# Residual rows and half of the gated tiles turned by VectorE through DRAM, with permuted features and channels, the decay's sums a step later, and one load for the small vectors

## The chip, the cores and the metric

The kernel runs on one core of a Trainium2 chip. The metric is the device time of one execution in microseconds (us). Inputs and weights lie in the core's HBM, laid out by the host beforehand (the function `_layout` of the kernel file), which isn't part of the time.

## The reference

Two layers over 256 context and 256 latent tokens of width 1024. Layer 0 mixes tokens with a Conformer convolution, layer 1 with a bidirectional chunkwise mLSTM (4 heads of 512); each is followed by a squared-ReLU MLP. Every sub-layer is modulated by adaLN vectors of `c` (latent) or `c_ctx` (context) and normalised behind its residual. Cut to what matters here:

```python
def conformer_conv(u, rows, w_pw1, b_pw1, w_dw, b_dw, ln_g, ln_b, w_pw2, b_pw2):
    a = u @ w_pw1 + b_pw1
    a = a[..., :CONV_DIM] * jax.nn.sigmoid(a[..., CONV_DIM:])     # the gated tiles
    ...                                                           # depthwise convolution of 31 taps along tokens
    a = jax.nn.silu(layer_norm(a + b_dw, ln_g, ln_b))
    return a @ w_pw2 + b_pw2

def mlstm_chunk_scan(q, k, v, i_pre, f_pre, state):
    lf = jax.nn.log_sigmoid(f_pre)
    ...
        bcum = jnp.cumsum(lfc, axis=-1)                           # the decay's sums
...
    h = layer_norm(ALPHA * h + g1 * y, ln1_g[i], ln1_b[i])        # ALPHA * h: the residual
```

## The kernel before, in words

Activations lie with features on the 128 partitions and tokens along the free axis: 8 tiles of 128 features by 512 tokens (256 context, 256 latent). Each fp32 product is three fp32r products of high and low halves (`mm3`: high by high, high by low, low by high, L182, L185, L186; `mm3t` with the operands' roles swapped, L213 to L215). The high half of a weight block of 128x1024 is a cast on ScalarE (L151), the low half a subtract on VectorE (L152); raw weights come in loads of 1 MB (`raw_load`, L145) on SyncE's queue SP, with three buffers.

The order of the work within an engine is fixed when the program is built, from the order of the code and the scheduler's own estimates; `tc.issue_after` ties an instruction behind another one. Each engine, and each queue, works in its own order.

**The start.** SP loads the small vectors `vecs` in two pieces: 64 columns ahead of all weights (L117, 32 KB), and the other 344 behind two feature tiles' loads (L657, 172 KB). The adaLN weights follow, and TensorE multiplies them with the conditioning at L344, once for each of eight feature tiles, in turn with the first four output tiles of the first pointwise product.

**The gated tiles.** The first pointwise product (`pw1_epi`) gives 16 output tiles, a gate and an up half for each `f` of eight: the sigmoid of the gate on ScalarE (L791), then bias and product on VectorE (L795), which gives 128 channels by 512 tokens. The convolution is done as Fourier transforms along tokens, so tokens must lie on the partitions: `turn` makes four 128x128 transposes on TensorE (L806) and one copy to the rows tile `A` by ScalarE (L807). Tiles 0 to 2 are put off to the next output tile (`turns`). The forward transform (`fwd`, L830 and L835) reads channels 0 to 511 of `A` (tiles 0 to 3) in its first half and 512 to 1023 in its second. The spectrum of the taps (L741) is a product with a table `tab` of cosines, which VectorE computes in the same stretch (L706 to L715).

**The residual rows.** Layer 1 continues in rows (tokens on partitions) after its output projection. Between the z projection (`up_z`) and the x projection (`up_x`), ScalarE scales and shifts the eight feature tiles (L1199), TensorE turns them (16 transposes, L1202), ScalarE copies them to a rows tile (L1204) and writes this to DRAM (`r_dr`, L1205, 1 MB). It is loaded again (L1573) at the output gate's second head half, `(h, d) == (0, 1)`. The epilogue of `up_x` is `x_epi`.

**The decay.** A string of names sets the order of the mLSTM's parts: a generator of main work (the output gate `gate_o`, attention `attend`, output projection `down`) and one of side work (`decay`, `guards`, `weights`), of which some steps are taken per step of the main one. A `yield` is the end of a step. `decay` makes `lf`, the log-sigmoid of the forget gates (last of it L1421), then on TensorE its sums (L1435 with triangles, L1436 with ones), and from these the running maximum `negm`. `gate_o` multiplies with `wo` in the three products of L213 to L215, and adds its bias on VectorE (L1588).

Of the kernel before, what the change touches and what calls it, by code (L numbers as in the profile page):

```python
# [21 lines left out]
C = 256  # L22
# [49 lines left out]
def hybrid_kernel(ctx: ExitStack, tc: tile.TileContext, xT, vecs_d, wdw_d, ada0_w, ada_w, wg_d, pw1a, pw1, pw2, w1_0, w2_0,  # L72
# [12 lines left out]
    def nm(s):  # L85
        uid[0] += 1
        return f"{s}_{uid[0]}"
# [3 lines left out]
    def tmp(tag, dt=F32):  # L91
        return tp.tile([P, T], dt, tag=tag, name=nm(tag), bufs={"E": 4, "S": 2, "L": 2, "F": 1}[tag])
# [8 lines left out]
    def psum(tag="mm"):  # L101
        return pp.tile([P, 512], F32, tag=tag, name=nm(tag), bufs={"mm": 3, "ln": 2, "fl": 1, "cv": 2}[tag])
# [551 lines left out]
    start1(0)  # L654
    idle(spare, 5)
    start0(1)
    nc.sync.dma_start(vecs[:, NV0:], vecs_d[:, NV0:])  # L657
    for f in range(DT):
        start2(f, (0,))
        if f + 1 < DT:  # L660
# [118 lines left out]
                              qtr.rearrange("p (b j c) -> p j b c", b=4, j=4)[:, :, :, 0:16])  # L779


    A = padp.tile([P, 4, D], F32, name="A")
# [18 lines left out]
    turns = []  # L801

    def turn(f, a):
        tr = psum("ln")
# [106 lines left out]
    def pw1_next(m, ps):  # L911
        while turns:
            turns.pop(0)()
        if m == 3:
            first.extend(ada_load(0, 4))
            ada_g1.mm(first, range(4))
        if m == 11:
            ada_s2.mm(half + ada_load(0, 6 + ada_s2.n, halves=(1,)))
            with tc.issue_after(mark["gate"]):
                nc.scalar.activation(warm, eps, AF.Sqrt)  # L920
        if m in (5, 6):
            with tc.issue_after(lastmm[0]):
# [265 lines left out]
    for _ in side:  # L1188
        pass

    def rows_tile():
        return xp.tile([P, 2, D], F32, tag="res", name=nm("res"), bufs=1)

    r_dr = dp.tile([P, 2, D], F32, name="r_dr")
    R = rows_tile()
    for f in range(0, DT, 2):
        t, tr = tmp("S"), psum("cv")
        for i in range(2):
            nc.scalar.activation(t[:, i * C:(i + 1) * C], x[f + i][:, HI], AF.Identity, scale=al[:, 0, f + i:f + i + 1],  # L1199
                                 bias=al[:, 1, f + i:f + i + 1])  # L1200
            for tt in range(2):
                nc.tensor.transpose(tr[:, tt * C + i * P:tt * C + (i + 1) * P],  # L1202
                                    t[:, i * C + tt * P:i * C + (tt + 1) * P], ident)
# [8 lines left out]
    def x_epi(m, ps):  # L1212
        pad = B("pad5")
        nc.gpsimd.memset(pad[:, :, 0:2], 0.0)
        nc.gpsimd.memset(pad[:, :, C + 2:C + 4], 0.0)
        mid = pad[:, :, 2:C + 2]
        nc.scalar.copy(mid, s2_(ps))
        nc.scalar.dma_start(xl_dr[m // 8][:, m % 8, :], pad[:, 1, 2:C + 2])
        hi, lo = XM(F32R), (X if m % 2 else U)(F32R)
        nc.scalar.copy(hi, ps)  # L1220
        nc.vector.tensor_tensor(s2_(lo), mid, s2_(hi.bitcast(F32)), op=ALU.subtract)
        xm.append((hi, lo))
        acc, sg = tmp("E"), tmp("E")
# [4 lines left out]
        nc.scalar.activation(sg, acc, AF.Silu)  # L1228
# [163 lines left out]
    def decay(_):  # L1392
# [565 lines left out]
def _cols(v):  # L1958
    return v.reshape(-1, P).T
# [6 lines left out]
def _layout(np, i):  # L1966
    g = {k: np.asarray(v) for k, v in i.items()}
    a, turned = {}, _turned(np)
    a["xT"] = np.concatenate([g["ctx"][0], g["x"][0]], axis=0).T
    vec = {  # L1970
        "c_ctx": _cols(g["c_ctx"]), "c": _cols(g["c"][0]),
        "b_pw1": _cols(g["conv_b_pw1"][0]),
        "cln_g": _cols(g["conv_ln_g"][0]), "cln_b": _cols(g["conv_ln_b"][0]),
        "b_pw2": _cols(g["conv_b_pw2"][0]), "b_conv": _cols(g["ml_b_conv"][0]),
        "w_conv": g["ml_w_conv"][0].T.reshape(ET, P, QTAP).transpose(1, 0, 2).reshape(P, ET * QTAP),
# [15 lines left out]
    pw1 = g["conv_w_pw1"][0].reshape(D, 2, DT, P).transpose(0, 2, 1, 3)[:, :, ::-1, :].reshape(D, 2 * D)  # L1991
# [16 lines left out]
    ab = g["ada_b"][1].reshape(6, D)  # L2008
# [25 lines left out]
```

## Time and profile before

| | |
|---|---|
| median of three runs | 1662.8 us (1662.76, 1662.8, 1665.79) |
| the profiled execution | 1665.14 us, its span 1663.4 us |
| TensorE busy | 1648.7 us, 8856 matmuls |
| VectorE, ScalarE busy | 1038.1 us, 734.6 us |
| granted TensorE clock | 0.999 |
| the transposes that the change takes from TensorE | 16 at L1202 (629.1 to 633.9 us), 16 of the 32 at L806 (50.5 to 143.9 us) |
| moved by DMA | 303.70 MB |

All times of rows are microseconds from the start of the span; the span lies in an execution that takes 1.7 us more. An engine's share of the span says how far it is from being the bound. A matmul's duration contains the pipeline's length, so matmuls that follow each other overlap in the rows, and the distance of their starts is what one costs in the stream. "A<-B" is a row's output and input by the names of the program.

### The profile page before, as it was taken

The page shows a single profiled execution, that of the slowest core. Times are in us where ns is not written, and L with a number is a line of the kernel's source. Part 1 is how long each engine was busy: PE and PEld are TensorE (multiplying, and loading weights), DVE is VectorE, ACT ScalarE, POOL GpSimd, SP SyncE. Part 2 cuts the span into 40 slices and gives each one's busy share as a digit, 9 for nine tenths or more (in the row PEclk, how much of TensorE's full clock was granted, in tenths as well). Part 3 has the DMA queues.
Part 4 walks back from the last instruction along what each step waited for, and adds up shares of the span by engine and source line. Part 5 has one row for each costly group of instructions (what it writes and reads, how often), then busy time and mean ns, then how long its engine had stood idle before and what let it go on. Part 6 is the DMA issues. An engine that isn't in the chain of part 4 may idle for free.

```text
span 1663.4 us, 22731 instructions
## 1 busy us (share of the span) xinstructions
PE 1648.7 (99%) x8856; PEld 1357.6 (82%) x8856; DVE 1038.1 (62%) x1863; ACT 734.6 (44%) x1182; POOL 14.4 (1%) x64
## 2 busy tenths in 40 slices
PE   9999999999999999999999999999999999999998
PEld 6665898888888998877787899888877888878886
DVE  6554895666535765762354753553489876776677
ACT  4313573232324476652233533442477654555453
POOL 0000000000000000000000000000000000000001
PEclk9999999999999999999999999999999999999999
DMA  9555223534324065557774852554465555675552
GB/s 353 208 210 214 92 75 111 167 123 148 136 101 152 4 228 194 184 196 266 278 259 146 302 179 79 179 194 144 148 240 197 203 215 203 250 284 183 178 194 85
DMA packets 74331, 303.70 MB, mean 183 GB/s; under 512 B 7694, under 2 KB 23858, under 8 KB 44144
## 3 DMA queue, kind: packets, MB, share of 16 engines
q1 hardware_dynamic: 56368, 286.49, 49.1%
q10 hardware_dynamic: 17856, 15.77, 2.8%
q8 instruction: 69, 1.13, 0.3%
q14 instruction: 38, 0.31, 0.1%
HBM read 285.42 MB, written 16.81 MB: 182 GB/s over the span
## 4 chain that ended last, share of the span: by engine, by line
PE 95%; DVE 2%; DMA 1%; ACT 1%; issue 0%; SPq 0%; DVEq 0%; ACTq 0%
PE mm L182 18%; PE mm L185 17%; PE mm L186 17%; PE mm L197 7%; PE mm L198 4%; PE mm L215 3%; PE mm L213 3%; PE mm L214 3%; PE cv L213 2%; PE cv L215 2%; PE cv L214 2%; PE fl L344 1%; PE ln L182 1%; PE cv L860 1%; PE ln L214 1%; PE ln L185 1%
## 5 line engine op out<-in xcount | busy, mean ns | idle before, releaser
L152 DVE TENSOR_TENSOR wl<-raw,wh 128x1024 fp32r<-128x1024 f32 x344 | 418.7, 1221 | 245.5 <-ACT wh L151 233.4
L151 ACT CAST wh<-raw 128x1024 fp32r<-128x1024 f32 x344 | 358.6, 1051 | 469.3 <-PE mm L185 244.4
L185 PE MATMUL mm<-u,wh 128*128 128x512 f32 (+1 forms) x808 | 291.5, 361 | 0.2 <-DVE u L604 0.2
L182 PE MATMUL mm<-u,wh 128*128 128x512 f32 (+1 forms) x680 | 243.8, 359 | 0.0
L186 PE MATMUL mm<-u,wl 128*128 128x512 f32 (+1 forms) x680 | 241.3, 355 | 0.0
L185 PEld LDWEIGHTS mm<-u,wh 128*128 128x128 f32 x808 | 152.7, 189 | 23.2 <-issue 1.0
L182 PEld LDWEIGHTS mm<-u,wh 128*128 128x128 f32 x680 | 128.4, 189 | 24.4 <-issue 6.3
L186 PEld LDWEIGHTS mm<-u,wl 128*128 128x128 f32 x680 | 128.5, 189 | 17.8
L213 PE MATMUL mm<-wh,xl 128*128 128x512 f32 x256 | 101.0, 395 | 0.7 <-DVE og L1588 0.7
L182 PE MATMUL mm<-xm,wh 128*128 128x512 f32 x256 | 101.0, 394 | 0.0
L215 PE MATMUL mm<-wl,xl 128*128 128x512 f32 x256 | 100.0, 393 | 0.0
L214 PE MATMUL mm<-wh,xl 128*128 128x512 f32 x256 | 99.9, 390 | 0.0
L186 PE MATMUL mm<-xm,wl 128*128 128x512 f32 x256 | 99.7, 389 | 0.0
L182 PE MATMUL mm<-hid,wh 128*128 128x512 f32 (+1 forms) x256 | 93.3, 364 | 0.0
L186 PE MATMUL mm<-hid,wl 128*128 128x512 f32 (+1 forms) x256 | 92.8, 363 | 0.0
L185 PE MATMUL mm<-hid,wh 128*128 128x512 f32 (+1 forms) x256 | 92.8, 363 | 0.0
L197 PE MATMUL mm<-x,wh 128*128 128x512 f32 x232 | 81.1, 398 | 0.0
L185 PE MATMUL mm<-qq,wh 128*128 128x272 f32 x256 | 73.9, 289 | 0.0
L182 PE MATMUL mm<-qq,wh 128*128 128x272 f32 x256 | 73.5, 288 | 0.0
L186 PE MATMUL mm<-qq,wl 128*128 128x272 f32 x256 | 73.5, 288 | 0.0
L197 PE MATMUL mm<-u,wh 128*128 128x512 f32 x192 | 68.6, 399 | 0.0
L1099 DVE SCALAR_TENSOR_TENSOR x<-mm,ada,x 128x256 f32<-128x256 f32 x64 | 28.5, 479 | 63.4 <-PE mm L186 63.4
(537 smaller groups left out, 3249.4 us busy)
## 6 DMA issues: line engine op xcount, KB each, us to landing
raw<-w SPq DMA_DIRECT2D x64, 1024.0 KB, 4.9
raw<-wo SPq DMA_DIRECT2D x32, 1024.0 KB, 4.9
raw<-ada_w SPq DMA_DIRECT2D x22, 1024.0 KB, 7.0
ar<-ada_w SPq DMA_DIRECT2D x80, 256.0 KB, 3.9
raw<-wv SPq DMA_DIRECT2D x16, 1024.0 KB, 8.0
raw<-wqT SPq DMA_DIRECT2D x16, 1024.0 KB, 5.7
raw<-wq SPq DMA_DIRECT2D x16, 1024.0 KB, 5.8
raw<-wk SPq DMA_DIRECT2D x16, 1024.0 KB, 5.2
```

The lines of the kernel that those rows point to most:

```text
L151: c = nc.scalar.copy(hi, src)
L152: lastsub[0] = nc.vector.tensor_tensor(lo, src, hi.bitcast(F32), op=ALU.subtract).ins
L182: a = nc.tensor.matmul(ps, wh, xh, start=start, stop=False)
L185: nc.tensor.matmul(ps, wh, xl, start=False, stop=False)
L186: lastmm[0] = nc.tensor.matmul(ps, wl, xh, start=False, stop=stop).ins
L197: todo = [lambda s_, e_: nc.tensor.matmul(ps, wh, r[0], start=s_, stop=e_), lambda s_, e_: nc.tensor.matmul(ps[:, :n], wl, r[0][:, :n], st ...
L198: lambda s_, e_: nc.tensor.matmul(ps[:, :n], wl, r[0][:, :n], start=s_, stop=e_)]
L213: nc.tensor.matmul(ps, xh, wh, start=start, stop=False)
L214: nc.tensor.matmul(ps, xl, wh, start=False, stop=False)
L215: nc.tensor.matmul(ps, xh, wl, start=False, stop=stop)
L344: a = mark_unit[0] = nc.tensor.matmul(ps[32 * j:32 * j + 32], cs[:, kt, 14 - 2 * v:46 - 2 * v], blocks[kt], start=first and kt < 4, stop=l ...
L1099: nc.vector.scalar_tensor_tensor(res[m][:, sl_], p_, g[:, m:m + 1], res[m][:, sl_], op0=ALU.mult, op1=ALU.add)
```

## The change

Six things, in one edit. (1) Features (of `x`, of the weights that make or read them, and of the vectors) and the channels of tiles 0, 1, 4 and 5 are permuted on the host in blocks of 32. A transpose of VectorE turns each 32x32 block by itself, and in the permuted order the blocks that it leaves lie so that one strided write to DRAM puts them in their rows. (2) Tiles 0, 1, 4 and 5 aren't turned by `turn`: VectorE transposes each (`vturn3`), and after the second of a pair ScalarE's queue writes the two in four DMAs (128 KB each, in runs of 64 elements) to `a_dr`; SP (first pair) and ScalarE's queue (second pair, at output tile 8 of those that follow) load them into `A`. Tile 2 alone is put off now. (3) The eight tiles of the residual are transposed by VectorE, 128x256 each, and four DMAs write them to `r_dr`, one in each of the first four epilogues of `up_x`. (4) The rows are loaded at `(1, 1)` of the output gate. (5) Two more `yield`s stand ahead of the decay's sums. (6) `vecs` is loaded in one piece of 204 KB ahead of all weights.

```diff
@@ -113,8 +113,7 @@
 
 
     vecs = con.tile([P, NV], F32, name="vecs")
-    NV0 = _OFF["ada_b1"][0]
-    nc.sync.dma_start(vecs[:, :NV0], vecs_d[:, :NV0])
+    nc.sync.dma_start(vecs, vecs_d)
 
...
     start0(1)
-    nc.sync.dma_start(vecs[:, NV0:], vecs_d[:, NV0:])
...
+    a_dr = [dp.tile([P, 4, 2 * P], F32, name=f"a_dr{h}") for h in range(2)]
...
-        if f < 3:
+        if f == 2:
             turns.append(lambda: turn(f, a))
+        elif f % 4 > 1:
+            turn(f, a)
         else:
-            turn(f, a)
+            vturn3(f, a)
...
+    def vturn3(f, a):
+        h, m = divmod(f, 4)
+        if m == 0:
+            three.append(rows_tile().rearrange("p a b -> p (a b)")[:, 0:8 * P].rearrange("p (t q m j) -> p t q m j", q=4, m=2, j=32))
+        vk = three[-1]
+        nc.vector.transpose(vk[:, :, :, m, :], a)
+        if m == 1:
+            for r in range(4):
+                nc.scalar.dma_start(a_dr[h][:, :, r * 64:r * 64 + 64].rearrange("(q j) t x -> j t q x", j=32),
+                                    vk[32 * r:32 * r + 32].rearrange("j t q m i -> j t q (m i)"))
+            if h == 0:
+                with tc.issue_after(loaded[0]):
+                    nc.sync.dma_start(A[:, :, 0:2 * P], a_dr[0])
...
         pw1_epi(m + KO0, ps)
+        if m == 8:
+            with tc.issue_after(mark["gate"]):
+                nc.scalar.dma_start(A[:, :, 512:512 + 2 * P], a_dr[1])
...
-    R = rows_tile()
+    vr = rows_tile().rearrange("p a (b m j) -> p a b m j", m=DT, j=32)
     for f in range(0, DT, 2):
-        t, tr = tmp("S"), psum("cv")
+        t = tmp("S")
         for i in range(2):
             nc.scalar.activation(t[:, i * C:(i + 1) * C], x[f + i][:, HI], AF.Identity, scale=al[:, 0, f + i:f + i + 1],
                                  bias=al[:, 1, f + i:f + i + 1])
-            for tt in range(2):
-                nc.tensor.transpose(tr[:, tt * C + i * P:tt * C + (i + 1) * P],
-                                    t[:, i * C + tt * P:i * C + (tt + 1) * P], ident)
-        nc.scalar.copy(R[:, :, f * P:(f + 2) * P], tr.rearrange("p (t c) -> p t c", t=2))
-    nc.scalar.dma_start(r_dr, R)
+            nc.vector.transpose(vr[:, :, :, f + i, :], t[:, i * C:(i + 1) * C])
...
+        if m < 4:
+            with tc.issue_after(o.ins):
+                nc.scalar.dma_start(r_dr[:, :, m * C:(m + 1) * C].rearrange("(q j) t x -> j t q x", j=32),
+                                    vr[32 * m:32 * m + 32].rearrange("j t q m i -> j t q (m i)"))
...
+        yield
+        yield
         yield
         yield
         bps = psum("ln")
...
-            if (h, d) == (0, 1):
+            if (h, d) == (1, 1):
                 with tc.issue_after(loaded[0]):
                     nc.sync.dma_start(R, r_dr)
...
+    xs = np.arange(D).reshape(4, DT, 32).transpose(1, 0, 2).reshape(D)
+    for n in ("conv_w_pw1", "mlp_w1", "ml_w_up"):
+        g[n] = np.concatenate([g[n][:1][:, xs], g[n][1:]])
...
+    glu = np.arange(D)
+    for h in (0, 512):
+        glu[h:h + 256] = h + np.arange(256).reshape(4, 2, 32).transpose(1, 0, 2).reshape(256)
```

**TensorE at the taps.** The rows are in program order, with the kernel's line, the output and its inputs (`mm` and `ln` are accumulators, `u` the modulated input, `wh` and `wl` a weight block's halves). Before, from the last matmuls of one output tile on:

```order
L186 MATMUL mm_604<-u_427,wl_650 128x512
L182 MATMUL mm_604<-u_473,wh_649 128x512
L185 MATMUL mm_604<-u_474,wh_649 128x512
L186 MATMUL mm_604<-u_473,wl_650 128x512
L182 MATMUL mm_684<-u_154,wh_688 128x512
L741 MATMUL ln_678<-L_575,tab 128x512
L741 MATMUL ln_681<-L_575,tab 128x512
L185 MATMUL mm_684<-u_155,wh_688 128x512
```

Now, from the same place on:

```order
L181 MATMUL mm_681<-u_154,wh_685 128x512
L184 MATMUL mm_681<-u_155,wh_685 128x512
L185 MATMUL mm_681<-u_154,wl_686 128x512
L181 MATMUL mm_681<-u_196,wh_685 128x512
L184 MATMUL mm_681<-u_197,wh_685 128x512
L185 MATMUL mm_681<-u_196,wl_686 128x512
L181 MATMUL mm_681<-u_242,wh_685 128x512
L184 MATMUL mm_681<-u_243,wh_685 128x512
L185 MATMUL mm_681<-u_242,wl_686 128x512
L181 MATMUL mm_681<-u_288,wh_685 128x512
L739 MATMUL ln_675<-L_574,tab 128x512
L739 MATMUL ln_678<-L_574,tab 128x512
```

Nine more matmuls of 512 columns of the next output tile stand ahead of the taps' product with `tab` (line 741 before, 739 now). The eight transposes of tiles 0 and 1, which stood further up (between the two output tiles before), are gone.

**VectorE at the taps.** Before, from the products that complete tiles 0 and 1 (L795; 797 now) on, with the low halves of weights (L152; 151 now) and the table's steps (L711 and L712; 709 and 710 now):

```order
L710 TENSOR_SCALAR tab<-F_532 128x384
L795 SCALAR_TENSOR_TENSOR E_596<-mm_106,vecs,E_596 128x512
L795 SCALAR_TENSOR_TENSOR E_599<-cv_108,vecs,E_599 128x512
L711 TENSOR_TENSOR F_533<-tab 128x384
L152 TENSOR_TENSOR wl_650<-raw_605,wh_649 128x1024
L152 TENSOR_TENSOR wl_689<-raw_686,wh_688 128x1024
L152 TENSOR_TENSOR wl_731<-raw_686,wh_730 128x1024
L712 TENSOR_SCALAR F_532<-F_533 128x384
L706 TENSOR_SCALAR F_546<-tab 128x256
```

Now:

```order
L708 TENSOR_SCALAR tab<-F_531 128x384
L797 SCALAR_TENSOR_TENSOR E_597<-mm_106,vecs,E_597 128x512
L797 SCALAR_TENSOR_TENSOR E_602<-cv_108,vecs,E_602 128x512
L812 STREAM_TRANSPOSE res_600<-E_597 128x16x32
L812 STREAM_TRANSPOSE res_600<-E_602 128x16x32
L151 TENSOR_TENSOR wl_647<-raw_614,wh_646 128x1024
L151 TENSOR_TENSOR wl_686<-raw_683,wh_685 128x1024
L151 TENSOR_TENSOR wl_728<-raw_683,wh_727 128x1024
L709 TENSOR_TENSOR F_532<-tab 128x384
L704 TENSOR_SCALAR F_545<-tab 128x256
L710 TENSOR_SCALAR F_531<-F_532 128x384
```

Two transposes stand ahead of three weight blocks, and the step of the table that stood right behind the products (L711) has gone behind those blocks.

**The decay on TensorE.** `wh` and `wl` are the halves of a `wo` block, `xl` the tokens' inputs. Before:

```order
L213 MATMUL mm_10689<-wh_10855,xl_10672 128x512
L214 MATMUL mm_10689<-wh_10855,xl_10672 128x512
L215 MATMUL mm_10689<-wl_10856,xl_10672 128x512
L213 MATMUL mm_10690<-wh_10855,xl_10669 128x512
L214 MATMUL mm_10690<-wh_10855,xl_10669 128x512
L1435 MATMUL ln_10750<-E_10714,tri 128x4x32
L215 MATMUL mm_10690<-wl_10856,xl_10669 128x512
L1436 MATMUL ln_10750<-E_10713,ones 128x4x32
L1435 MATMUL ln_10750<-E_10714,tri 128x4x4
L1436 MATMUL ln_10750<-E_10713,ones 128x4x4
L213 MATMUL mm_10690<-wh_10855,xl_10672 128x512
```

Now, with the same sums in lines 1455 and 1456, from two matmuls before the place in the block at which they stood:

```order
L212 MATMUL mm_10670<-wh_10820,xl_10649 128x512
L213 MATMUL mm_10670<-wh_10820,xl_10649 128x512
L214 MATMUL mm_10670<-wl_10821,xl_10649 128x512
L212 MATMUL mm_10670<-wh_10820,xl_10652 128x512
L213 MATMUL mm_10670<-wh_10820,xl_10652 128x512
L214 MATMUL mm_10670<-wl_10821,xl_10652 128x512
L212 MATMUL mm_10669<-wh_10853,xl_10655 128x512
L1455 MATMUL ln_10748<-E_10694,tri 128x4x32
L213 MATMUL mm_10669<-wh_10853,xl_10655 128x512
L1456 MATMUL ln_10748<-E_10693,ones 128x4x32
L1455 MATMUL ln_10748<-E_10694,tri 128x4x4
L1456 MATMUL ln_10748<-E_10693,ones 128x4x4
```

The sums with the triangle stood behind the second matmul of a group of three, four matmuls ahead of the block's end; now they stand behind the first matmul of the next block, five of 512 columns later.

**The decay on VectorE.** The chain of `lf` (`E` and `L` are small tiles of 128x144 here) and the weight blocks between its steps. Before:

```order
L152 TENSOR_TENSOR wl_10880<-raw_10877,wh_10879 128x1024
L1417 RECIPROCAL E_10713<-E_10713 128x144
L152 TENSOR_TENSOR wl_10910<-raw_10877,wh_10909 128x1024
L1418 TENSOR_TENSOR E_10713<-E_10713 128x144
L1419 TENSOR_TENSOR E_10714<-E_10713,E_10714 128x144
L1423 MEMSET E_10713 128x144
L1421 TENSOR_TENSOR E_10714<-E_10714 128x144
L1426 COPY E_10713<-E_10714 128x32
L1426 COPY E_10713<-E_10714 128x4
L1427 TENSOR_TENSOR E_10713<-E_10713,E_10714 128x32
```

Now:

```order
L151 TENSOR_TENSOR wl_10854<-raw_10851,wh_10853 128x1024
L1435 RECIPROCAL E_10693<-E_10693 128x144
L151 TENSOR_TENSOR wl_10876<-raw_10851,wh_10875 128x1024
L1436 TENSOR_TENSOR E_10693<-E_10693 128x144
L151 TENSOR_TENSOR wl_10918<-raw_10915,wh_10917 128x1024
L1437 TENSOR_TENSOR E_10694<-E_10693,E_10694 128x144
L1441 MEMSET E_10693 128x144
L1439 TENSOR_TENSOR E_10694<-E_10694 128x144
L1444 COPY E_10693<-E_10694 128x32
L1444 COPY E_10693<-E_10694 128x4
L1445 TENSOR_TENSOR E_10693<-E_10693,E_10694 128x32
```

One more weight subtract stands between L1418 and L1419 (1436 and 1437 now), ahead of the last step of `lf` (L1421; 1439 now).

More of the change, by code (lines that the diff above doesn't have):

```diff
@@ L779, in wgq_last, with rows_tile @@
                               qtr.rearrange("p (b j c) -> p j b c", b=4, j=4)[:, :, :, 0:16])
+    def rows_tile():
+        return xp.tile([P, 2, D], F32, tag="res", name=nm("res"), bufs=1)
     A = padp.tile([P, 4, D], F32, name="A")
+    a_dr = [dp.tile([P, 4, 2 * P], F32, name=f"a_dr{h}") for h in range(2)]
     Y = [[U() for _ in range(2)] for _ in range(4)]
@@ L795, in pw1_epi @@
         nc.vector.scalar_tensor_tensor(a, ps, V("b_pw1", f), a, op0=ALU.add, op1=ALU.mult)
-        if f < 3:
+        if f == 2:
             turns.append(lambda: turn(f, a))
-        else:
-            turn(f, a)
-    turns = []
+        elif f % 4 > 1:
+            turn(f, a)
+        else:
+            vturn3(f, a)
+    turns, three = [], []
+    def vturn3(f, a):
[11 more added lines that the diff above has]
+                    nc.sync.dma_start(A[:, :, 0:2 * P], a_dr[0])
     def turn(f, a):
@@ L1189, in hybrid_kernel @@
         pass
-    def rows_tile():
-        return xp.tile([P, 2, D], F32, tag="res", name=nm("res"), bufs=1)
     r_dr = dp.tile([P, 2, D], F32, name="r_dr")
-    R = rows_tile()
+    vr = rows_tile().rearrange("p a (b m j) -> p a b m j", m=DT, j=32)
     for f in range(0, DT, 2):
-        t, tr = tmp("S"), psum("cv")
+        t = tmp("S")
         for i in range(2):
@@ L1227, in x_epi @@
                                            op0=ALU.mult, op1=ALU.add)
-        nc.scalar.activation(sg, acc, AF.Silu)
+        o = nc.scalar.activation(sg, acc, AF.Silu)
         nc.scalar.dma_start(xc_dr[m // 4][:, m % 4, :], sg)
+        if m < 4:
+            with tc.issue_after(o.ins):
+                nc.scalar.dma_start(r_dr[:, :, m * C:(m + 1) * C].rearrange("(q j) t x -> j t q x", j=32),
+                                    vr[32 * m:32 * m + 32].rearrange("j t q m i -> j t q (m i)"))
         sk = tmp("E")
@@ L1968, in _layout @@
     a, turned = {}, _turned(np)
-    a["xT"] = np.concatenate([g["ctx"][0], g["x"][0]], axis=0).T
+    xs = np.arange(D).reshape(4, DT, 32).transpose(1, 0, 2).reshape(D)
+    for n in ("conv_w_pw1", "mlp_w1", "ml_w_up"):
+        g[n] = np.concatenate([g[n][:1][:, xs], g[n][1:]])
+    for n in ("conv_w_pw2", "mlp_w2", "conv_b_pw2", "ln1_g", "ln1_b", "ln2_g", "ln2_b"):
+        g[n] = np.concatenate([g[n][:1][..., xs], g[n][1:]])
+    ab = g["ada_b"][1].reshape(6, D)
+    for n in ("ada_w", "ada_b"):
+        t = g[n].reshape(2, -1, 6, D)
+        g[n] = np.concatenate([t[:1][..., xs], np.concatenate([t[1:, :, :2][..., xs], t[1:, :, 2:]], axis=2)]).reshape(g[n].shape)
+    a["xT"] = np.concatenate([g["ctx"][0], g["x"][0]], axis=0).T[xs]
+    glu = np.arange(D)
+    for h in (0, 512):
+        glu[h:h + 256] = h + np.arange(256).reshape(4, 2, 32).transpose(1, 0, 2).reshape(256)
     vec = {
         "c_ctx": _cols(g["c_ctx"]), "c": _cols(g["c"][0]),
-        "b_pw1": _cols(g["conv_b_pw1"][0]),
+        "b_pw1": _cols(g["conv_b_pw1"][0].reshape(2, D)[:, glu].reshape(-1)),
         "cln_g": _cols(g["conv_ln_g"][0]), "cln_b": _cols(g["conv_ln_b"][0]),
@@ L1990, in _layout @@
     a["wg_d"] = wg.reshape(3, ET, P, 16).transpose(0, 2, 1, 3).reshape(3, P, 256)
-    pw1 = g["conv_w_pw1"][0].reshape(D, 2, DT, P).transpose(0, 2, 1, 3)[:, :, ::-1, :].reshape(D, 2 * D)
+    pw1 = g["conv_w_pw1"][0].reshape(D, 2, D)[:, :, glu].reshape(D, 2, DT, P).transpose(0, 2, 1, 3)[:, :, ::-1, :].reshape(D, 2 * D)
     a["pw1a"] = pw1[:, :512].reshape(DT, P, 512)
```

1 line of the change is left out of this document (removed).

## The prediction

> **What bounds the kernel now.** The page comes first: its span, its engine table and its chain of work.
>
> ```profile
> span 1663.4 us, 22731 instructions
> PE 1648.7 (99%) x8856; PEld 1357.6 (82%) x8856; DVE 1038.1 (62%) x1863; ACT 734.6 (44%) x1182; POOL 14.4 (1%) x64
> PE 95%; DVE 2%; DMA 1%; ACT 1%; issue 0%; SPq 0%; DVEq 0%; ACTq 0%
> ```
>
> TensorE is busy 99% of the span, and 95% of the chain that ended last lies on it. What shortens TensorE's own stream shortens the kernel by about as much; work on VectorE, ScalarE and the queues costs nothing until TensorE waits for it. The second view is the list of all waits of TensorE (what it waited for: total us, times, longest):
>
> ```profile
> PE ln L1435 <- DVE E L1421: 1.6, 1, 1.6
> PE fl L344 <- DMA raw<-ada_w: 1.4, 2, 1.2
> PE cv L176 <- DVE ones L130: 1.1, 1, 1.1
> PE mm L213 <- DVE og L1588: 0.7, 1, 0.7
> PE ln L741 <- issue: 0.6, 1, 0.6
> ```
>
> These five add up to 5.4 us, and the list goes on with shorter ones only. So waits can give back some 6 us, and the change touches four of them: the first adaLN weights (1.4), the taps (0.6), the decay's sums (1.6) and, behind the sums, the gate's first addition (0.7). Everything else must come out of instructions that leave TensorE.
>
> **Part 1: 32 transposes leave TensorE.** Sixteen turn the residual rows (L1202), sixteen the GLU tiles 0, 1, 4 and 5 (half of L806's 32). What one costs is not its duration: starts lie closer together than that. I take it from a stretch without a wait, the end of the z projection to the first matmuls of the x projection (rows: start us, duration, instruction), and then the same stretch in groups (instruction, count, busy us and mean ns, idle before):
>
> ```profile
> 628.95 0.28 PE L186 MATMUL mm<-u,wl 128*128 128x256 f32 x1
> 629.07 0.71 PE L1202 MATMUL cv<-ident,S 128*128 128x128 f32 x5
> ...
> 634.28 0.40 PE L182 MATMUL mm<-u,wh 128*128 128x512 f32 x1
> 634.52 0.39 PE L185 MATMUL mm<-u,wh 128*128 128x512 f32 x1
> ...
> 639.96 0.39 PE L185 MATMUL mm<-u,wh 128*128 128x512 f32 x1
> ```
>
> ```profile
> L1202 PE MATMUL cv<-ident,S 128*128 128x128 f32 x16 | 2.6, 272 | 0.0
> L182 PE MATMUL mm<-u,wh 128*128 128x512 f32 x6 | 2.5, 422 | 0.0
> L186 PE MATMUL mm<-u,wl 128*128 128x512 f32 x5 | 2.1, 427 | 0.0
> L185 PE MATMUL mm<-u,wh 128*128 128x512 f32 x5 | 2.0, 408 | 0.0
> ```
>
> From 628.95 to 634.28 are 5.33 us. In it stand one 256-wide matmul (start to start 629.07 − 628.95 = 0.12) and 15 of the 512-wide (6 + 5 + 5, less the one at 634.28), which follow each other every 0.227 us where nothing comes between (the 24 steps from 634.52 to 639.96 take 5.44). 5.33 − 0.12 − 15 × 0.227 = 1.81 us for 16 transposes, 0.113 each. The GLU's first eight, with two 512-wide matmuls in the stretch:
>
> ```profile
> 50.29 0.39 PE L186 MATMUL mm<-u,wl 128*128 128x512 f32 x1
> 50.52 1.03 PE L806 MATMUL ln<-ident,E 128*128 128x128 f32 x8
> ...
> 51.62 0.40 PE L185 MATMUL mm<-u,wh 128*128 128x512 f32 x1
> ```
>
> 51.62 − 50.29 − 2 × 0.227 = 0.88 us for eight, 0.110 each. So 32 × 0.113 = **3.6 us** leave TensorE (3.5 by the other row). None of the stretches has a wait, so no stall hides there that could come back.
>
> The duration row speaks otherwise: each transpose is shown with 272 ns, and 32 of them would be 8.7 us. The Trainium skill (TensorE: Matmul & The Clock Gate, Part 4: PE-mode transpose) puts a transpose in a kernel at about 275 ns; the trace agrees with the duration, but the starts show that durations overlap. By that price the sum below would be 5.1 us larger; I give it a rival's chance.
>
> **Part 2: the same work on VectorE, ScalarE and the queues.** The rows to price it with: a stream transpose of 128x512; busy time in the GLU's stretch and at the residual's (us of the stretch, then PE, PEld, DVE, ACT); four strided writes issued by ScalarE, and how long such writes take to land; the weight cast behind the new writes; and three points of TensorE: the first reader of the GLU rows, the old transposes of tile 5, the reader of the second half.
>
> ```profile
> L1261 DVE STREAM_TRANSPOSE res<-vt x16: 702/706/714, 735.1 to 914.9; 128x512 f32<-128x512 f32 x16
> 45.00:150.00 105.00, 104.40 (x474) 67.31 (x472) 54.41 (x93) 27.59 (x36) 1.99 (x8) 1.00 0.53 189
> 620.00:640.00 20.00, 20.00 (x134) 18.25 (x134) 7.45 (x9) 13.21 (x23) 0.00 (x0) 1.00 0.77 289
> 915.69 2.78 ACTq L1265 DMA_DIRECT2D v_dr<-res x4
> DMA to landing us min/median/max: 3.6/6.3/10.3
> 61.35 1.05 ACT L151 CAST wh<-raw 128x1024 fp32r<-128x1024 f32 x1 [8.98 <-DMA raw<-pw]
> 75.84 1.13 PE L830 MATMUL mm<-A,ge 128*128 128x512 f32 x2
> 119.96 0.60 PE L806 MATMUL ln<-ident,E 128*128 128x128 f32 x4
> 145.05 1.13 PE L830 MATMUL mm<-A,ge 128*128 128x512 f32 x2
> ```
>
> VectorE gets four transposes of 0.71 us in 105 us with 50.6 us idle, and eight of 128x256 at the residual, where it idles 12.5 of 20 us; that shape isn't in the trace, at most 0.71 and at least half of a proportional share, 0.18 each, so 1.4 to 5.7 us; I take 0.36, 2.9 us. Both fit. ScalarE loses eight copies and gains twelve issues; four cost 2.78 us (915.69), and it is idle 77 of 105 us, 8.98 of them ahead of the cast at 61.35. TensorE sees none of that as long as it stays in these gaps. Value 0; price if the cover goes: see the slower rival.
>
> The round trip through DRAM has to end before the forward transform reads A at 75.84. Tiles 0 and 1 are complete when their old transposes begin (50.52), so turned by 51.9; the four issues end at 54.7, and landing takes 3.6 to 10.3, so to 58.3 or 65.0; the read (512 KB) takes the same once more, 61.9 to 75.3. It is in time at both ends, by 0.5 us at the worse one. Tile 5 is complete at 119.96: one more transpose, issues and two landings end at 130.7 to 144.1, ahead of 145.05. Value 0, upper end 1 us each.
>
> A rule speaks against these writes: the runs that reach DRAM are 256 bytes long (64 elements). The Trainium skill (DMA: Bandwidth & Descriptors, Specifications) names 512 B as the least for line rate, below which a read-modify-write is done. No row here has these writes; if it doubled the transfer, 128 KB would count like the 256 KB of v_dr above, whose landing I have already used.
>
> **Part 3: vecs in one load at the start.** The second load (172 KB), the DMA rate, and the two groups of adaLN matmuls that waited for weights:
>
> ```profile
> GB/s 0 16 82 336 418 348 445 444 410 381 392 460 442 371 459 424 426 373 447 418 412 381 463 440 375 393 449 430 381 453 422 424 381 393 127 131 451 410 8 98
> vecs<-vecs_d SPq DMA_DIRECT2D x1, 172.0 KB, 7.9
> 6.89 1.07 PE L344 MATMUL fl<-raw,cs 128*32 128x256 f32 x16 [1.18 <-DMA raw<-ada_w]
> 10.63 1.07 PE L344 MATMUL fl<-raw,cs 128*32 128x256 f32 x16 [0.24 <-DMA raw<-ada_w]
> ```
>
> The queues run at about 420 GB/s, so 172 KB put ahead of the first weights push them back by 0.41 us. TensorE waits for exactly these at 6.89 and again at 10.63, so it pays: **+0.4 us**. The list of waits has only these two of the kind; from the third on the weights are early, and by then the same bytes have been moved as before. Bounds 0 (the first microseconds of the queues are far from full: 16, then 82 GB/s) and 0.6.
>
> **Part 4: the taps.** VectorE now turns tiles 0 and 1 before it finishes the table `tab`, on which the taps' matmul waited (the 0.6 above ends with the row shown here):
>
> ```profile
> 57.29 0.42 DVE L715 SCALAR_TENSOR_TENSOR tab<-F,tab 128x256 f32<-128x256 f32 x1
> ```
>
> Two transposes put `tab` 1.4 us later. TensorE's list has 9 more 512-wide matmuls ahead of the taps (2.04 us) and eight transposes fewer (0.88): it arrives 1.16 later. The wait becomes 0.6 + 1.4 − 1.16 = 0.8, or **+0.2** (−0.6 to +0.8).
>
> **Part 5: the decay's sums.** A weight subtract on VectorE ahead of the sums, the sums on TensorE (1.63 us of waiting, ended by `lf`, VectorE's L1421), and the gate's addition on VectorE behind them:
>
> ```profile
> 1214.25 1.19 DVE L152 TENSOR_TENSOR wl<-raw,wh 128x1024 fp32r<-128x1024 f32 x1
> 1216.40 0.49 PE L1435 MATMUL ln<-E,tri 128*128 128x128 f32 x2 [1.63 <-DVE E L1421]
> 1248.55 0.67 DVE L1588 TENSOR_TENSOR og<-mm,bo 128x512 f32<-128x512 f32 x1
> ```
>
> In the change's order five more 512-wide matmuls stand ahead of the sums, 1.13 us. Alone that leaves 0.5 of the 1.63. But VectorE's order moves too: one more weight subtract (1.2 us) now stands between the two steps that finish `lf`, because the scheduler finds a later program place for the sums. Then `lf` is 1.2 later, TensorE 1.13 later: **+0.1**. Bounds −1.1 (the subtract finds an idle gap) and +1.2. What follows the chain (maximum, exponentials) shifts by about 1.5 us against TensorE; for the gate's addition at 1248.55 VectorE's order has one subtract fewer ahead of it, so it should come 1.2 us earlier and its wait of 0.7 go: **−0.7**. Bounds −0.7 and +2 (the attention's products, later on TensorE, wait for the subtract that slipped behind the addition; about 1.7 subtracts of 1.2).
>
> The R load of 1 MB goes to a later gate head. The casts at the decay wait for DMA, TensorE doesn't; R is read after the last head. Value 0.
>
> **The sum.** −3.6 + 0.4 + 0.2 + 0.1 − 0.7 = −3.6 us. The profiled execution took 1665.14 us (span 1663.4, 1.7 around it), 2.3 above the median of 1662.8; against itself it becomes 1661.5, and against the median **1659.2 us**. About 0.2% or 3.3 us is what a measurement of this kernel can tell from no change, so the forecast stands just on the side of faster.
>
> **Rivals.**
> - The decay's wait goes as well. For it: the five matmuls suffice if the added subtract runs in one of VectorE's gaps. Against it: VectorE works in order, and it ended the wait already. The decay's term becomes −1.1 instead of +0.1, and if the taps' wait goes as well, −0.6 instead of +0.2: 1659.2 − 1.2 − 0.8 = 1657.2.
> - The gain is eaten by waits of VectorE (taps +0.8 instead of +0.2, decay +1.2 instead of +0.1, products +2 instead of −0.7): 1659.2 + 0.6 + 1.1 + 2.7 = 1663.6; in part, anything from 1660 on. For it: all three waits in question end on VectorE, which gets more work just ahead of them. Against it: VectorE is idle 38% of the span.
> - Slower: ScalarE is held by its own writes. A queue that takes a write only when the one before has landed would keep ScalarE from the next weight cast. It needs to be free at 61.35 for that cast. Four landings of 6.3 us from 51.9 end at 77.1, 15.8 us late: 1659.2 + 15.8 = 1675.0. With landings of 3.6 they end at 66.3, 5.0 us late, and little more than the gain is gone; from 6.9 us beyond 61.35 (the 3.6 gained and 3.3 more) it is slower by over 0.2%. Against it: four v_dr writes were issued in 2.78 us without a landing between them.
> - The transposes were worth their duration: 1659.2 − 5.1 = 1654.1. Against it: the stretch of 5.33 us.
>
> **Chances.** Forecast 0.42 (half of it above the 1659.5 that 0.2% means), the decay's wait gone 0.17, gain eaten 0.27, slower 0.12, full durations 0.02. Faster: 0.25 + 0.17 + 0.02 = 0.44; same: 0.17 + 0.27 = 0.44; slower 0.12. The range reaches from 1656.8 (the first rival, with vecs at 0 instead of +0.4) to 1664.0 (the second, with vecs at +0.6, rounded up) and leaves out the slower rival and the full durations, and a little of the tails.
>
> **What would show it.** Right: TensorE's matmul count down by 32, the stretch at 629 shorter by 1.8 us, the first adaLN wait 1.6 instead of 1.2, the decay's wait between 1.6 and 1.9, no entry for `og`. Wrong: a wait of L830 on a DMA into A, ScalarE idle behind a write, or a weight cast at 61 that starts later than before.

## The result: slower by 0.15%, and the profile after

| kernel | median us | runs | ratio to before [95%] |
|---|---|---|---|
| before | 1663.51 | 14 | |
| changed | 1666.57 (1664.46 to 1669.03) | 14 | 1.0015 [1.0008, 1.0022] |

By the ratio the change costs 2.5 us (3.1 by the medians) where a gain of 3.6 was forecast. Ratios here and below leave out one execution, of the experiment e7, that took 4442 us. The profiled execution of the changed kernel took 1664.94 us, 1.6 us under its median, and that of before 1665.14, 1.6 above; so the two profiles show where time moves, and the medians how much it is. The page after, span, engines and chain:

```profile
span 1663.2 us, 22679 instructions
PE 1647.8 (99%) x8824; PEld 1355.2 (81%) x8824; DVE 1042.6 (63%) x1875; ACT 730.4 (44%) x1174; POOL 14.3 (1%) x64
PE 92%; DVE 4%; DMA 3%; ACT 1%; issue 1%; SPq 0%; DVEq 0%; ACTq 0%
```

The 32 matmuls are gone (8856 to 8824), yet TensorE's busy time falls by 0.9 us only, and its share of the chain from 95% to 92%: DMA and VectorE have come in. The list of TensorE's waits after:

```profile
PE fl L765 <- DMA raw<-wqT: 3.4, 2, 2.4
PE cv L175 <- DVE ones L129: 1.1, 1, 1.1
PE mm L212 <- ACT wh L150: 0.8, 1, 0.8
PE ln L739 <- DVE tab L713: 0.5, 1, 0.5
PE mm L212 <- DVE og L1608: 0.4, 1, 0.4
...
PE fl L343 <- DMA raw<-ada_w: 0.2, 1, 0.2
...
PE ln L1455 <- DVE E L1439: 0.2, 1, 0.2
```

The waits that the prediction spoke of have all shrunk. The largest is new: `wgq`, a product of a gate weight with wqT (L765, 767 before), which stands in no part of the change. To see where the gain goes, the same matmul is followed in both profiles, at three places: the last of the z projection, then the 97th and the 169th of the 512-wide products with a weight's low half behind it. First before, then after, with three of the wgq rows that have come between:

```profile
628.95 0.28 PE L186 MATMUL mm<-u,wl 128*128 128x256 f32 x1
...
696.63 0.39 PE L186 MATMUL mm<-u,wl 128*128 128x512 f32 x1
...
749.78 0.40 PE L186 MATMUL mm<-xm,wl 128*128 128x512 f32 x1
```

```profile
626.42 0.28 PE L185 MATMUL mm<-u,wl 128*128 128x256 f32 x1
...
692.30 0.39 PE L185 MATMUL mm<-u,wl 128*128 128x512 f32 x1
...
699.80 1.05 PE L765 MATMUL fl<-raw,wgq 128*32 128x512 f32 x2 [2.36 <-DMA raw<-wqT]
...
713.10 1.07 PE L765 MATMUL fl<-raw,wgq 128*32 128x512 f32 x8
...
720.92 1.06 PE L765 MATMUL fl<-raw,wgq 128*32 128x512 f32 x8 [1.08 <-DMA raw<-wqT]
...
750.92 0.39 PE L185 MATMUL mm<-xm,wl 128*128 128x512 f32 x1
```

The changed kernel is 2.53 us ahead at the end of the z projection, 4.33 ahead in the x projection (the 1.8 of the residual's transposes, as worked out), and 1.14 behind at 750. So 5.5 us are lost between 692 and 751, and 3.4 of them are the wait on wqT. Before, the first of these products stood at 734.35, inside the v projection, in pairs of steps of 1.92 us (734.35 and 747.35). By the last rows shown both kernels have done four steps, so the 5.5 us aren't work that was only moved ahead; but after they came in five pieces of about 1.06 us, which is some 1.5 us more.

### The profile page after: what moved, and what is told of

It is laid out like the page before. It is cut to its first block, busy times and chain, and to the rows that moved or that the text cites. A ratio compares the mean times of both kernels' runs of the same rounds, so it can differ in the third digit from the quotient of the medians.

```text
span 1663.2 us, 22679 instructions
## 1 busy us (share of the span) xinstructions
PE 1647.8 (99%) x8824; PEld 1355.2 (81%) x8824; DVE 1042.6 (63%) x1875; ACT 730.4 (44%) x1174; POOL 14.3 (1%) x64
## 4 chain that ended last, share of the span: by engine, by line
PE 92%; DVE 4%; DMA 3%; ACT 1%; issue 1%; SPq 0%; DVEq 0%; ACTq 0%
PE mm L181 17%; PE mm L184 17%; PE mm L185 17%; PE mm L196 7%; PE mm L197 4%; PE mm L212 3%; PE mm L214 3%; PE mm L213 3%; PE cv L212 2%; PE fl L343 1%; PE cv L214 1%; PE cv L213 1%; DVE wl L151 1%; PE fl L765 1%; PE ln L181 1%; PE cv L878 1%
```

## The experiments

Each ratio is to executions of the kernel before on the same chip, measured side by side.

| kernel | median us | before | ratio [95%] |
|---|---|---|---|
| e1 wgq tied to its old place | 1666.04 | 1664.19 | 1.0010 [1.0002, 1.0019] |
| e2 residual writes at once | 1665.13 | 1664.19 | 1.0008 [0.9999, 1.0017] |
| e3 residual part alone | 1667.51 | 1664.19 | 1.0021 [1.0011, 1.0030] |
| e4 gated tiles alone | 1661.92 | 1664.19 | 0.9985 [0.9976, 0.9993] |
| e5 change, writes not tied | 1662.12 | 1664.00 | 0.9988 [0.9979, 0.9997] |
| e6 change, writes by GpSimd | 1660.53 | 1664.00 | 0.9978 [0.9970, 0.9987] |
| e7 yields alone | 1664.48 | 1664.00 | 1.0006 [0.9997, 1.0015] |
| e8 R load alone | 1663.63 | 1664.00 | 0.9999 [0.9990, 1.0008] |
| e9 e6 with serial order | 1678.27 | 1664.31 | 1.0082 [1.0068, 1.0096] |
| e10 both transposes, GpSimd, nothing else | 1660.42 | 1664.31 | 0.9975 [0.9965, 0.9985] |
| e11 e10 with vecs in one | 1661.42 | 1664.31 | 0.9980 [0.9971, 0.9989] |
| e12 e10, all new writes by GpSimd | 1659.90 | 1664.31 | 0.9969 [0.9958, 0.9981] |

**First theory: the moved wgq products (e1 to e4).** The first theory was that the scheduler moved these products forward for no reason that the chip has, and that they cost what they wait. e1 ties them back:

```diff
         for j in range(4):
+          with tc.issue_after(lastmm[0]):
             nc.tensor.matmul(wqs[0][32 * j:32 * j + 32, :], ...
```

> The whole change, with the sixteen products of wgq with wqT tied behind the matmul that precedes them in the code, so that TensorE meets them in pairs of steps inside the v projection, as before the change. Theory A (the change's loss is these products, which moved some 30 us ahead on TensorE, wait there for wqT and come one step at a time): 5.4 us come back up to 750 us, of which the decay's sums may take up to 1.6 again because TensorE arrives earlier; no wait on wqT; 1660.5 to 1662.5, against 1663.5 before and 1666.6 changed. Theory B (the residual's four writes in the x projection disturb the weights, the order of wgq doesn't matter): 1666 as the change, with a wait in the x projection. Theory C (the loss is in the moved R load or the start): 1666, no wait on wqT.

1666.04: nothing came back. The products are at their old place and wqT isn't waited for; TensorE's list shows what came instead:

```profile
PE mm L181 <- ACT xm L1235: 4.0, 4, 1.2
```

Four waits of 1.2 us at most, 7 us apart, on ScalarE's cast to `xm`, the second of the two readings that empty an accumulator of the x projection. So the wgq products had only filled gaps that were there anyway: theory A falls, and the question is why ScalarE is late. e2 issues the four writes right behind the transposes instead of in the epilogues:

```diff
             nc.vector.transpose(vr[:, :, :, f + i, :], t[:, i * C:(i + 1) * C])
+    for m in range(4):
+        nc.scalar.dma_start(r_dr[:, :, m * C:(m + 1) * C]..., vr[32 * m:32 * m + 32]...)
```

> The whole change, but the four writes of the residual rows are issued right behind the eight transposes instead of one in each of the first four epilogues of the x projection; this alone puts the wgq products back to their place in the v projection. Theory A: as e1, 1660.5 to 1662.5. Theory B: also 1661, so e1 tells the two apart. If four writes of 256 KB at once hold ScalarE or the weight loads: a wait of TensorE just behind 627 us, 1663 to 1666.

Its order has no wait on `xm`, nor on wqT, but one of 2.8 us on a weight cast. TensorE's row and ScalarE's:

```profile
635.14 0.65 PE L181 MATMUL mm<-u,wh 128*128 128x512 f32 x1 [2.83 <-ACT wh L150]
```

```profile
627.94 2.01 ACTq L1221 DMA_DIRECT2D r_dr<-res  x3
632.35 0.59 ACT L1234 COPY pad<-mm 128x512 f32<-128x512 f32 x1 [5.08 <-PE mm L185]
...
634.06 3.88 ACT L150 CAST wh<-raw 128x1024 fp32r<-128x1024 f32 x4
```

The three issues end at 629.95; as I read the rows, the wait comes from the order, which puts four casts behind the first epilogue, so that ScalarE idles 5.08 us in front of it while casts are outstanding. The 1665.1 doesn't tell A from B; it shows that a write's place decides which order ScalarE gets. The parts by themselves, e3 (residual) and e4 (gated tiles):

> The kernel before with the residual part alone (transposes on VectorE, writes in the x projection's epilogues, permuted features). Its order has the wgq products early, as the change. Theory A: -1.8 us for sixteen transposes, +5.4 for wgq, up to -1.5 where the decay's wait absorbs it: +2 to +3.6, 1665.5 to 1667. Theory C: -1.8, 1661.7.

> The kernel before with the gated tiles' part alone. Its order has the wgq products at their old place. Theory A and B: -1.8 us for sixteen transposes, with the taps' wait within 0.5 of before: 1661.2 to 1662.2. If the round trip through DRAM or VectorE costs something: 1663.5 or more, with a wait of TensorE between 50 and 150 us.

e3 is slower by 3.3 us of medians and e4 faster by 2.3: the residual part holds the whole loss, and the gated tiles bring their 1.8 and a little. Together they are +1.0, against +2.5 for the whole change; the intervals, about 1.5 us to either side of each part, cover the difference.

**Second theory: ScalarE's order in the x projection (e5, e6, e9).** The epilogue of an x tile has a chain through two engines: ScalarE copies the accumulator (L1231), makes a start value from it (L1238), VectorE adds four taps to it (L1240), ScalarE takes Silu (L1242). Before, ScalarE between two Silus (those lines are 1217, 1224, 1226, 1228 there):

```profile
694.35 0.63 ACT L1228 ACTIVATE E<-E 128x512 f32<-128x512 f32 x1 [1.61 <-DVE E L1226]
...
695.80 0.80 ACT L1224 ACTIVATE E<-pad,vecs 128x512 f32<-128x512 f32 x1
...
696.50 0.56 ACT L1217 COPY pad<-mm 128x512 f32<-128x512 f32 x1
...
700.26 0.64 ACT L1228 ACTIVATE E<-E 128x512 f32<-128x512 f32 x1 [1.74 <-DVE E L1226]
```

and after:

```profile
694.83 0.63 ACT L1242 ACTIVATE E<-E 128x512 f32<-128x512 f32 x1 [1.96 <-DVE E L1240]
695.37 0.57 ACT L1231 COPY pad<-mm 128x512 f32<-128x512 f32 x1
...
696.28 0.80 ACT L1238 ACTIVATE E<-pad,vecs 128x512 f32<-128x512 f32 x1
...
701.75 0.63 ACT L1242 ACTIVATE E<-E 128x512 f32<-128x512 f32 x1 [2.97 <-DVE E L1240]
```

The copy in these rows isn't of the same tile as the start value beside it: counted from the first row of each kind, 695.37 is the eleventh copy and 696.28 the eighth start value, so copies run three tiles ahead. Before, a copy stands behind a start value and ahead of the Silu that waits for VectorE; after, it stands behind that Silu and ahead of the next start value. The start value comes 1.45 us behind Silu in both orders. What makes the turn shown longer (from Silu to Silu 6.92 us against 5.91) is on VectorE: the low half of a weight (L152; 151 after) stood behind the last tap, and now stands ahead of it. Before, then after:

```profile
698.69 1.53 DVE L1226 SCALAR_TENSOR_TENSOR E<-pad,vecs,E 128x512 f32<-128x512 f32 x2
700.14 1.22 DVE L152 TENSOR_TENSOR wl<-raw,wh 128x1024 fp32r<-128x1024 f32 x1
```

```profile
699.17 0.75 DVE L1240 SCALAR_TENSOR_TENSOR E<-pad,vecs,E 128x512 f32<-128x512 f32 x1
699.83 1.22 DVE L151 TENSOR_TENSOR wl<-raw,wh 128x1024 fp32r<-128x1024 f32 x1
700.97 0.75 DVE L1240 SCALAR_TENSOR_TENSOR E<-pad,vecs,E 128x512 f32<-128x512 f32 x1
```

So Silu waits 2.97 instead of 1.74 us for the last tap, by the 1.22 of the subtract. The 5.91 is one of the shorter turns; in the mean a turn takes 7.0 us before as well (16 Silus, 644.76 to 750.03), longer than the 24 matmuls x 0.227 = 5.4 us that TensorE needs for a tile. That cost nothing before, because the copies didn't keep to the turns; sometimes two of them stand between the same two Silus. After, the last eight of the 16 copies stand behind a Silu, one to a turn, and so does the second copy (nine in all, as the expectations say, but not all nine at the end); before, four of 16, three of them the last. The copies of before, of after and of e5 (below):

```profile
L1217 ACT COPY pad<-mm x16: 563/578/589, 636.5 to 721.5; 128x512 f32<-128x512 f32 x16
L1231 ACT COPY pad<-mm x16: 565/568/591, 632.9 to 731.5; 128x512 f32<-128x512 f32 x16
L1231 ACT COPY pad<-mm x16: 565/588/591, 633.8 to 719.3; 128x512 f32<-128x512 f32 x16
```

They spread over 85.0 us before, 98.6 after and 85.5 in e5; over 98.3 and 100.5 in e1 and e3, which have the tie too. After, the last eight come 7.8 us apart (676.99 to 731.52), and TensorE stops when its accumulators aren't emptied, as e1's waits on `xm` show. The writes are tied behind Silu (`issue_after(o.ins)`); e5 drops only the tie, and e6 gives the writes to GpSimd's queue:

```diff
         if m < 4:
-            with tc.issue_after(o.ins):
-                nc.scalar.dma_start(r_dr...)
+            nc.scalar.dma_start(r_dr...)          # e5; in e6 nc.gpsimd.dma_start
```

> The whole change, but the residual's four writes are not tied behind the epilogue's Silu (the same writes, in the same four epilogues, on the same queue). Without the tie ScalarE's order in the x projection is that of before again for most epilogues (the next start value ahead of the Silu that waits for VectorE), and the wgq products stand in the v projection. Theory D (the tie puts Silu ahead of the next copy in nine of the last epilogues, ScalarE and VectorE then work by turns, 6.9 us a tile against TensorE's 5.4, and TensorE waits, or gets the wgq products as a filler): no wait on xm or wqT, TensorE 4 us ahead of before at 750; 1660 to 1661.5 against 1664.2 before. Theory E (four more issues of 0.58 us on ScalarE and eight transposes on VectorE overload the x projection by themselves): waits on xm or wh of 2 to 4 us stay; 1664 to 1666.

> The whole change, but the residual's four writes are issued by GpSimd in the same four epilogues, without a tie; ScalarE issues none. Theory D: as e5, 1660 to 1661.5. Theory E: if the issues on ScalarE are what costs, this is 2 us faster than e5; if VectorE's transposes are, both stay at 1664 to 1666.

The tie alone is worth 4.5 us (1.0015 to 0.9988; the intervals lie apart). Moving the four writes off ScalarE is worth 1.6 more (1662.12 to 1660.53, measured side by side: each of e5's eleven executions is slower than e6's median); as the orders differ a little between the two, the 1.6 isn't shown to be the issues' time alone. In e5 the waits on `xm` and wqT are gone. What is left on a weight's low half is short, and e6 has even less:

```profile
PE mm L185 <- DVE wl L151: 0.8, 2, 0.4
```

```profile
PE mm L185 <- DVE wl L151: 0.2, 1, 0.2
```

To show that an order costs by itself, and not something that goes with the tie, e9 puts a serial order into the quickest version so far without moving any work. It isn't the order of the changed kernel, as its expectation has it, but a stricter one: each copy stands behind the Silu of the tile just before, so that copy, start value, taps and Silu of one tile end before the next is copied.

```diff
-        nc.scalar.copy(mid, s2_(ps))
+        with tc.issue_after(silu[-1]) if silu else nullcontext():
+            nc.scalar.copy(mid, s2_(ps))
...
         o = nc.scalar.activation(sg, acc, AF.Silu)
+        silu.append(o.ins)
```

> e6 with nothing but an order added: each epilogue's copy of its accumulator on ScalarE is tied behind the Silu of the tile before, so that all 16 epilogues of the x projection stand in the order that nine have in the changed kernel. No write, no transpose differs from e6. Theory D: 6.9 us a tile against 5.4, 15 x 1.5 = 22 us less what the three accumulator banks and the gap to the v projection absorb (in the changed kernel nine tiles, 13 us, gave 5.4, so some 8): +10 to +20 us, 1670 to 1680. Theory E (not the order but the issues and transposes cost): 1660.5 as e6.

1678.27 against e6's 1660.53, inside the range of theory D and far from E. The 16 copies spread over 113.7 us (634.3 to 748.0). So an order alone can cost this much; what the changed kernel's own order costs is shown by e5. VectorE's order moved in e9 too (the weight's low half stands ahead of the last two taps), so no run tells the copies' place on ScalarE from the subtract's place on VectorE. The waits of both kinds come back together:

```profile
PE mm L181 <- ACT xm L1235: 8.0, 5, 1.8
PE fl L765 <- DMA raw<-wqT: 4.2, 2, 2.9
```

The wgq products moved forward here too, though nothing ties them: they follow from the order.

**The rest (e7, e8, e10 to e12).** e7 adds the two yields to the kernel before, e8 moves the R load there, e10 takes both transposes with the residual's writes by GpSimd and leaves out yields, R load and vecs, e11 adds vecs, e12 gives e10's gated writes to GpSimd as well.

> The kernel before with the two yields alone. My prediction: the sums' wait stays at 1.6 to 1.9, the gate's addition loses its 0.7: -0.6 us, 1663.6 against 1664.2. Rival: the sums' wait falls to 0.2 as in the changed kernel: -1.6 or more, 1662.5. Other rival: the later wait of 0.8 on a cast near 1414 us comes with the yields: nothing gained.

> The kernel before with the residual rows loaded at head 1, second half, instead of head 0. My prediction: 0 (1664.2). Rival: the casts of wo at the decay no longer wait for the 1 MB, lf comes earlier, and the wait of 1.6 falls to 0.5: 1663. Other rival: the wait of 0.8 on a cast near 1414 us is due to this: 1665.

> The kernel before with the gated tiles' part and the residual part, the residual's writes issued by GpSimd; vecs in two loads, no yields, the R load at head 0. Theory D, by the sum of the parts: -1.8 - 1.8 - what the taps pay: 0.9980 of before, 1660.7. Against e6 (0.9978) it prices yields, R load and vecs together: equal within 0.7 us by e7 and e8.

> e10 with vecs in one load. My prediction for the start: +0.4 us against e10, the first wait on adaLN weights 1.6 instead of 1.2. Rival: the second SP issue that goes and fewer transfers in flight make up for it: 0 or -0.3.

> e10 with the gated tiles' eight writes issued by GpSimd too, so ScalarE issues none of the new writes. If ScalarE's issues cost as they did between e5 and e6 (1.6 us for four): 1 us better than e10. If the gated stretch has the cover that I gave it (ScalarE idle 77 of 105 us): the same as e10 within 0.5.

In e7 neither the sums nor the gate's addition is in TensorE's list, but a wait of 0.8 on a cast of wo is new (at 1258.69, not at the 1414 that its expectation names); together nothing that can be told from no change. e8 is 0.9999. e10 (0.9975) and e6 (0.9978) agree, so yields, R load and vecs together bring nothing measurable. Vecs in one load (e11 against e10) is 1.0 us slower by medians, with intervals that overlap: my +0.4 is neither shown nor refuted. e12 is 0.5 us under e10, again within the intervals. It is the quickest kernel of the study, 0.9969 [0.9958, 0.9981], so faster than before and than the change.

## Why the prediction was wrong, step by step

- **Part 1, right.** 1.8 us at the residual (2.53 to 4.33 us ahead). For the gated tiles e4 gives 2.3, at 1.8 forecast. The durations' price, 8.7 us or 4.35 for each half, is refuted by both; so the 275 ns of the Trainium skill (TensorE: Matmul & The Clock Gate, Part 4: PE-mode transpose) was here a duration and not what a transpose costs in a stream, 0.11 us.
- **Part 2, the step that failed: "TensorE sees none of that as long as it stays in these gaps. Value 0".** I looked for cover for the new work in the 20 us around its old place, where VectorE had 12.5 us idle, and priced the four writes by their issue. They stand in the x projection, from 638 to 667 us. There a tie to Silu decided in which order ScalarE's and VectorE's programs were written, and that order cost 4.5 us; the writes' place on ScalarE's queue cost 1.6 more. e3 shows the size by itself: +3.3 us where −1.8 was forecast. The order of both kernels was there to be compared: in it TensorE's first wgq product stands some 145 matmuls earlier, ScalarE's copies stand behind Silu, and VectorE's subtract ahead of the last tap. I compared the orders only at the places that the diff names.
- **The round trip and the transposes' price, right.** 128x256 took 0.445 us (0.36 taken, 0.18 to 0.71 the bounds), on VectorE at 617 to 622 and waited for by none; A's rows were in time.

```profile
L1219 DVE STREAM_TRANSPOSE res<-S x8: 403/445/447, 617.7 to 621.9; 128x256 f32<-128x256 f32 x8
```

- **Part 3, open.** The waits on adaLN weights are 0.2 in all in this profile (1.6 forecast for the first alone), but 1.4, 1.0, 0.7 and 0.6 in profiles of the old start (before, e3, e7, e8), not in the list of e4 and e10 with the same start, and 0.9 in e11 with the new one: a single profile can't carry it.
- **Part 4, close.** 0.5 us of wait at the taps, 0.8 forecast, 0.6 before.
- **Part 5, wrong.** It took the wait of 1.6 at the sums for a property of the kernel's order, but the profiles with the same order don't repeat it. In the one of before the casts ahead of `lf` waited 3.21 us for a load of wo:

```profile
1207.03 2.00 ACT L151 CAST wh<-raw 128x1024 fp32r<-128x1024 f32 x2 [3.21 <-DMA raw<-wo]
```

  In e3 and e4, which have neither the yields nor the moved R load and the same order of these steps, the same casts waited 1.47 and 1.58, and the sums 0.2 and 0.3. So little was there to gain; why the load came late in the one execution is open. The added subtract doesn't come from the sums' later place either: it stands between the two steps in e8 (R load alone) and not in e7 (yields alone). The addition's wait is 0.4, not 0. A new wait of 0.8 on a cast stands at 1414; it is in every kernel that moves both transposes, with yields or without (e10 to e12), and in none of e3, e4, e7 and e8, and why is open. By e7, −0.6 isn't borne out and no gain can be shown.
- **The rivals.** "The gain is eaten" came true in its direction, by an order of two engines and at another place, and went past the rival's 1663.6. The slower rival, ScalarE held until its writes land, isn't seen. ScalarE did stand idle once for 3.3 us in the gated stretch, but behind the issue of its four writes (47.79 to 50.96; the next activation starts at 51.00), and without a cost: TensorE's list has no entry for it. The profile puts this to the write:

```profile
ACT E L793 <- DMA a_dr<-res: 3.3, 1, 3.3
```

- **The sum.** With the writes off ScalarE the change is what I had forecast: e6 has 0.9978, and 1659.2 / 1662.8 = 0.9978. So the gain of the transposes was right, and one unpriced stretch turned it into a loss. That the sum is met to 0.0001 is luck: e6's interval is 0.9970 to 0.9987, and the four small terms cancel in the forecast (+0.4 + 0.2 + 0.1 − 0.7), so they aren't borne out by it. The chances have a slip: half of 0.42 is 0.21, where the sum for faster takes 0.25.

## What to carry to other kernels

When a change adds an instruction with a tie to an engine that works in order, compare the whole program's order on every engine, not only around the diff, and look for instructions that moved though the change doesn't name them: here the moved wgq products were the sign, and not the cause, of an epilogue whose copies had come to wait for Silu. An engine that is busy 44% of the span (52% of the stretch from 676 to 731 us) can still be the bound of a stage, if its instructions and another engine's form a chain per tile that is longer than TensorE's time for the tile, and the instruction that frees TensorE's accumulator is tied to that chain. A wait that one profile shows may belong to that execution: look for it in a second one before pricing it. A queue's issue belongs on an engine that nothing waits for; here that was worth 1.6 us for four issues in the x projection, and nothing that can be told from no change for eight in the gated stretch (e12).

## What the runs showed of the hardware that I had not expected

- A column-tiled wgq step of TensorE costs the same whether one of its four products is issued or all: 699.80 with 1.05 us for the one that the order has there, 713.10 with 1.07 for four; the next matmul starts 0.98 and 1.00 us later. Splitting a step is therefore paid in full.
- In several of the profiled executions the granted clock fell at about 60 us, to 0.50 in two-microsecond slices, right behind the taps' wait. The rows of 56 to 60 and 60 to 64 us for before, and then for e8 (the third number from the end is the granted clock):

```profile
56.00:60.00 4.00, 3.42 (x11) 1.66 (x10) 2.28 (x5) 0.00 (x0) 0.86 (x4) 1.00 0.34 123
60.00:64.00 4.00, 4.00 (x19) 3.27 (x18) 1.23 (x1) 2.65 (x4) 0.00 (x0) 1.00 0.29 80
```

```profile
56.00:60.00 4.00, 3.41 (x11) 1.56 (x9) 1.82 (x4) 0.00 (x0) 0.44 (x3) 0.94 0.27 91
60.00:64.00 4.00, 4.00 (x13) 3.17 (x12) 1.25 (x2) 3.15 (x4) 0.00 (x0) 0.64 0.28 76
```

  By estimate it costs about 1.7 us (4 x 0.36 and 4 x 0.06, if TensorE is the bound all that time). It is seen in e3, e7 and e8, which have the gated tiles of before, and in e4 to e6, which have those of the change, and not in before, the change, e1 and e2. So it may be a part of the spread of 3 to 4 us between executions, and is one more reason to take medians for a change of this size. What brings it on, no run here shows.
- The gated tiles' writes (128 KB in 256-byte runs) landed in 2.6 to 11.2 us, 7.8 in the median; the residual's (256 KB in 1 KB runs) in 3.5 to 4.1. That agrees in direction with the Trainium skill (DMA: Bandwidth & Descriptors, Specifications), which wants at least 512 B; the two stood beside different loads, so the runs don't separate the length of the runs from the traffic.
